# Two transformer layers on one core: the sums of x1, the scaling of its rows and the inner operand parts of the feed-forward at other places in the program

## The chip, the core and the metric

The kernel runs on one core of one Trainium2 chip. The metric is the device time of one execution in microseconds (us), and of several executions the median. A core has a matrix engine (PE in the profile; its weight loads are PEld), a vector engine (DVE), a scalar engine (ACT), a general engine (POOL), and a queue engine that only issues transfers (SP). Each engine takes its instructions strictly in the order of its own list; engines wait for each other by semaphores. PE reads its operands from the on-chip memory SBUF and writes into eight accumulation banks; ACT and DVE read the banks back.

## The reference

Two layers run over 512 positions of 1024 channels. Each has a token mixer of three branches, and then the part that matters here: a norm, a gated feed-forward and a second norm.

```
mix = merged @ w_out[l]
x   = layer_norm(DEEPNORM_ALPHA * x + mix, ln1_g[l], ln1_b[l])
u   = x @ w_ffn_in[l];  u_gate, u_up = split(u)       # 1024 x 2*2816
ffn = (silu(u_gate) * u_up) @ w_ffn_out[l]            # 2816 x 1024
x   = layer_norm(DEEPNORM_ALPHA * x + ffn, ln2_g[l], ln2_b[l])
```

All arithmetic is float32, and the kernel keeps it so.

## The kernel before, in words

**Pairs.** PE multiplies in a shorter format. So every operand is carried as a pair: a high part `hi` (a cast, on ACT) and a low part `lo` (the source minus the high part, on DVE). One product step is three matmuls (`mm3`, L122 to L124): high by high, low by high, high by low. `split` makes a pair from a source (`part_hi` L106 and L108, `part_lo` L112 and L114).

**Products by seven.** Most of the feed-forward is not multiplied plainly. A problem of two by two blocks is computed with seven block products in place of eight, by Winograd's scheme; the names of the seven are m1, m2, y, x, g, h and v. Each needs block sums of both operands. On the weight side `Adds` and `Chain` form these sums in the staging buffers of the weights: with a DVE addition (L241, L246), or with a second load that accumulates onto the buffer (`more`, issued on POOL's queue). On the activation side `Quarters.turned` (L316 to L319) forms four sums of the quarters of x1, transposed, and splits them into the pairs `s12` and `s43`.

**The inner side** (x1 by `w_ffn_in`) has 22 tiles of 128 hidden columns. Sixteen are done by four such problems (`ffn_problem`, four tiles each). Two plain tiles come ahead of them (`u_ffn_first`, tiles 16 and 17), and four more (`u_ffn`, tiles 18 to 21) are put between later products. **The outer side** (hidden by `w_ffn_out`) has two problems, the groups 0 and 1 (`fout_items`), and a rest. The operand parts of an outer problem are made by `Hidden`: its methods y, m1, m2, x, g, v and h form a block sum of the hidden values and split it into the pairs `hq`.

**What sets the order.** The program is a list of items, each with the weights that it needs and a function that emits its products. `run_items` fetches weights until three stand ready, and calls the item. A fetch emits the load (on SP's queue), the high part (L292 or L154, ACT) and the low part (L293 or L155, DVE). Other work is hung on an item as groups of functions: `between()` pops the next group, and an item calls it after each of its products. So in `item(*pr[name], [], todo)` the empty group is popped after the first product and `todo` after the second. From this program order a scheduler makes the list of each engine; it may move instructions past each other where their data allow it.

**Around the change.** In `u_ffn_first` the two plain tiles are multiplied in halves of the positions: first positions 0 to 255 for eight k steps, with a hook ahead of the fifth step that emits the last transposes of x1 (`transposes(3)`, `to_T(1)`), then positions 256 to 511 tile by tile. `ffn_done` makes the hidden pair of a tile. `x1_sums` emits for each of four k the four sums of `turned`, two high parts and two low parts. `natural(t)` scales and shifts one block of 128 rows of x1 (four DVE operations over 128x512: L549, L550) and stores it (two transfers on SP's queue); those rows are the residual of the second norm. `load_res` loads them again as eight pieces of 256 KB, and `plus` adds the outer products to them on DVE. `REST` is 16, `GROUPS` is `[(0, 4), (8, 4)]`; group 0 reads the hidden values of the inner problems 0 and 1.

Of the kernel before, what the change touches and what calls it, by code (L numbers as in the profile page):

```python
# [20 lines left out]
NT = S // P  # L21
KT = D // P
# [28 lines left out]

GROUPS = [(0, 4), (8, 4)]
REST = 16


@with_exitstack
def trunk(ctx, tc, x_in, xT_in, w_in, ret_norm_g, da_norm_g, lq1, lk1, lq2, lk2, w_a, w_b, w_c, b_merge, w_out,
# [13 lines left out]
    saved = [dram.tile([S, D], F32, name=f"saved{i}") for i in range(2 * DEPTH - 1)]  # L71
# [287 lines left out]
    def proj_T(act, wt, c0, nk=KT, ps=None, half=None):  # L359

        ps = bank("pt") if ps is None else ps
        sl = slice(0, S) if half is None else slice(256 * half, 256 * half + 256)
        for k in range(nk):
            a = act[k]
            mm3(ps[:, sl], wt.hi[:, k, c0:c0 + P], wt.lo[:, k, c0:c0 + P], a.hi[:, sl], a.lo[:, sl],
                k == 0, k == nk - 1)
        return ps
# [188 lines left out]
    def item(specs, fn, *groups):  # L556

        items.append((specs, fn, groups))
# [3 lines left out]
    def between():  # L562

        if pending:
            for fn in pending.pop(0):
                fn()
# [54 lines left out]
    def layer(l):  # L621
# [7 lines left out]
        v = {}  # L629
# [520 lines left out]
        x1, x1f = {}, {}  # L1150
# [5 lines left out]
        def load_res(src):  # L1156
            x1["z"] = [[g(name="z") for _ in range(2)] for _ in range(NT)]
            for t in range(NT):
                load_rows(x1["z"][t], src[P * t:P * t + P])
# [58 lines left out]
        def x1_sums():  # L1218
            for k in range(4):
                x1q[k] = Quarters(x1T[k], x1T[k + 4])  # L1220
                x1q[k].turned(x1f.pop(k), x1f.pop(k + 4))

        def u_ffn_first(ids):
            def fn(*wts):
                n = len(ids)
                pg, pu = [bank("pt") for _ in range(n)], [bank("pt") for _ in range(n)]
                proj_T_half0(x1T, [(wts[i], P * j, p[i]) for i in range(n) for j, p in enumerate((pg, pu))],
                             {KT // 2: lambda: (x1["n"].transposes(3), x1["n"].to_T(1))})
                for i in range(n):
                    proj_T(x1T, wts[i], 0, ps=pg[i], half=1)  # L1230
                    proj_T(x1T, wts[i], P, ps=pu[i], half=1)
                    ffn_done(ids[i], pg[i], pu[i])
                    if i == 0:
                        x1_sums()
                for t in range(NT):
                    x1["n"].natural(t)
            return [ffn_spec(i) for i in ids], fn

        def u_ffn(i):
            def fn(wt):  # L1240
                pg = proj_T(x1T, wt, 0)
                pu = proj_T(x1T, wt, P)
                ffn_done(i, pg, pu)
            return [ffn_spec(i)], fn

        def ffn_problem(p):

            hv = Adds(w_ffn_in[l], 0, 4, (512 * p, FFN + 512 * p))
            Z, Y, t = [None] * 2, [None] * 2, {}

            def it(name, use):
                def fn(wt):
                    for b in range(2):
                        use(b, functools.partial(product_T, x1q, name, b, wt))
                        between()
                return [getattr(hv, name)], fn  # L1260

            def copy(to, b, ps):
                t[to, b] = g(name="f" + to)
                nc.scalar.copy(t[to, b], ps)

            def gated(src):
                th = g(name="fth")
                nc.scalar.activation(th, src, AF.Tanh, scale=0.5)
                nc.vector.scalar_tensor_tensor(th, th, 1.0, src, op0=ALU.add, op1=ALU.mult)
                return th  # L1270

            def m1(b, run):
                Z[b] = run()
                copy("m", b, Z[b])

            def m2(b, run):
                m = t.pop(("m", b))
                nc.vector.tensor_add(m, m, run())
                unit[p, 0, b] = gated(m)

            def y(b, run):
                Y[b] = run()

            def x(b, run):
                copy("u", b, run(Z[b], False))

            def gg(b, run):
                copy("w", b, run(Z[b], False))
                w = t["w", b]
                nc.vector.tensor_add(w, w, Y[b])  # L1290

            def h(b, run):
                th = unit[p, 1, b] = gated(run(Z[b], False))
                nc.vector.tensor_mul(th, th, t.pop(("w", b)))

            def v(b, run):
                u, th = t.pop(("u", b)), unit[p, 0, b]
                nc.vector.tensor_add(u, u, run(Y[b], False))
                nc.vector.tensor_mul(th, th, u)

            use = {"m1": m1, "m2": m2, "y": y, "x": x, "g": gg, "h": h, "v": v}
            return {"a": hv.ahead_a, "c": hv.ahead_c, **{k: it(k, fn) for k, fn in use.items()}}
# [68 lines left out]
        def fout_items(gi):  # L1371

            r0, kh = GROUPS[gi]
            hv = Chain(w_ffn_out[l], r0, kh)
            Z, Y, hd = [None] * 2, [None] * 2, {}

            def begin():
                hd["h"] = Hidden(r0 // 4)
                if gi == 0:
                    load_res(saved[2 * l])  # L1380
                    x2["fresh"] = {(t, hf) for t in range(NT) for hf in range(2)}

            def part(name):
                return lambda: getattr(hd["h"], name)()

            def run(name, j, wt, *to):
                return product([hd["h"].row(k) for k in range(kh)], name, j, wt, *to)

            def it(name, use):
                def fn(wt):  # L1390
                    for j in range(2):
                        use(j, functools.partial(run, name, j, wt))
                        between()
                return [getattr(hv, name)], fn

            def y(j, run):
                Y[j] = run()
                plus(2 + j, 1, Y[j], ALU.subtract)

            def m1(j, run):  # L1400
                Z[j] = run()
                plus(j, 0, Z[j], ALU.add)

            def m2(j, run):
                plus(j, 0, run(), ALU.add)

            def x(j, run):
                plus(j, 1, run(Z[j], False), ALU.subtract)

            def gg(j, run):  # L1410
                plus(2 + j, 1, run(Z[j], False), ALU.subtract)

            def v(j, run):
                plus(j, 1, run(Y[j], False), ALU.subtract)

            def h(j, run):
                plus(2 + j, 0, run(Z[j], False), ALU.add)

            use = {"y": y, "m1": m1, "m2": m2, "x": x, "g": gg, "v": v, "h": h}
            return {"a": hv.ahead_a, "c": hv.ahead_c, "begin": begin, "part": part,  # L1420
                    **{k: it(k, fn) for k, fn in use.items()}}

        def fout_rest(hf):
# [32 lines left out]

            return [([sp], block(kb)) for kb, sp in enumerate(specs)] if hf == 0 else [(specs, chase)]

        probs = [ffn_problem(p) for p in range(REST // 4)]
        outs = [fout_items(gi) for gi in range(len(GROUPS))]  # L1460
        item(*u_ffn_first([REST, REST + 1]), [probs[0]["a"], probs[0]["c"]])
        for p, pr in enumerate(probs):
            nxt = probs[p + 1] if p + 1 < len(probs) else outs[0]
            for name in ("m1", "m2", "y", "x", "g", "h", "v"):
                todo = {"g": [nxt["a"]], "v": [nxt["c"]]}.get(name, [])
                if nxt is outs[0]:
                    todo = todo + {"v": [nxt["begin"], nxt["part"]("y"), nxt["part"]("m1")]}.get(name, [])
                item(*pr[name], [], todo)
        rest = list(range(REST + 2, FT))
        for gi, o in enumerate(outs):  # L1470
            nxt = outs[gi + 1] if gi + 1 < len(outs) else None
            order = ("y", "m1", "m2", "-", "x", "g", "v", "-", "h")
            names = [n for n in order if n != "-"]
            for name in order:
                if name == "-":
                    item(*u_ffn(rest.pop(0)))
                    continue
                n = names.index(name) + 2
                todo = [o["part"](names[n])] if n < len(names) else []
                if nxt:  # L1480
                    todo += {"v": [nxt["a"]], "h": [nxt["c"], nxt["part"]("m1")]}.get(name, [])
                    if name == "v":
                        todo += [nxt["begin"], nxt["part"]("y")]
                item(*o[name], todo)
# [61 lines left out]
```

## Time and profile before

| what | us |
|---|---|
| median of three runs | 1926.54 (1925.36 to 1927.0) |
| the profiled execution, its own time | 1925.41 |
| its span, first to last instruction | 1923.6 |
| PE busy | 1885.2 (98%) |
| PEld busy | 1640.2 (85%) |
| DVE busy | 1388.2 (72%) |
| ACT busy | 963.6 (50%) |
| POOL busy | 101.5 (5%) |
| granted PE clock, mean | 0.99 of full |

Times inside the profile count from the first instruction. A wait row says which instruction an engine stood in front of, which instruction released it, the sum of the waits in us, how many there were and the longest. A row of the stretches view gives, for a stretch of time, the busy time of each engine with the number of its instructions, then the granted PE clock, the share of the transfer engines that was busy, and what they moved. A timeline row gives start, duration, engine, source line, operation and tiles, and behind it in brackets the idle time of the engine ahead of it with what ended it. Durations of neighbours on one engine can overlap by some 0.1 us, so the step from one to the next is read from their starts. The program's two layers show the same stretches about 957 us apart.

### The profile page before, as it was taken

How to read it: one execution, taken by the hardware profiler on the slowest of the kernel's cores; microseconds unless marked ns; L12 is line 12 of the kernel's file. 1: busy time of each engine (PE TensorE's matmuls, PEld its weight loads, DVE VectorE, ACT ScalarE, POOL GpSimd, SP SyncE). 2: the span in 40 equal slices, each digit the busy share in tenths (PEclk: the TensorE clock that was granted, in tenths of full speed). 3: DMA queues.
4: the chain of work that ended last, by engine and by line, in shares of the span. 5: the costliest groups of instructions: out<-in, count | busy, mean ns of one | idle time of the engine just before them, and what ended most of it. 6: DMA issues, size and time to landing. Idle time of an engine off the chain costs nothing. (4 is left out here: it accounts for less than half of the span.)

```text
span 1923.6 us, 26474 instructions
## 1 busy us (share of the span) xinstructions
PE 1885.2 (98%) x10354; PEld 1640.2 (85%) x10354; DVE 1388.2 (72%) x2111; ACT 963.6 (50%) x1559; POOL 101.5 (5%) x117
## 2 busy tenths in 40 slices
PE   9999999999999899899999999999999998999998
PEld 7788888888888899888898788888888888998886
DVE  5878866677666977777578788566675759777766
ACT  5555555576534544444255556455765344444441
POOL 0000000000001000010000000000000000000000
PEclk9999999999999899999999999999999998999999
DMA  8585443332264575975556844522422646769851
GB/s 277 168 265 152 133 158 115 99 121 78 72 213 110 155 196 154 252 187 152 153 171 174 254 125 142 185 84 94 132 66 71 218 106 177 175 175 241 197 153 44
DMA packets 221746, 297.85 MB, mean 155 GB/s; under 512 B 9534, under 2 KB 116148, under 8 KB 221620
## 3 DMA queue, kind: packets, MB, share of 16 engines
q1 hardware_dynamic: 198388, 250.01, 39.3%
q0 software_dynamic: 23232, 46.14, 13.8%
q8 instruction: 81, 1.33, 0.3%
q14 instruction: 45, 0.37, 0.1%
HBM read 273.00 MB, written 23.12 MB: 154 GB/s over the span
## 5 line engine op out<-in xcount | busy, mean ns | idle before, releaser
L122 PE MATMUL pt<-xTh,wh 128*128 128x512 f32 (+1 forms) x1456 | 506.1, 348 | 0.4 <-ACT wh L154 0.3
L123 PE MATMUL pt<-xTl,wh 128*128 128x512 f32 (+1 forms) x1456 | 502.5, 345 | 1.9 <-DVE xTl L112 1.9
L124 PE MATMUL pt<-xTh,wl 128*128 128x512 f32 (+1 forms) x1456 | 502.2, 345 | 0.0
L293 DVE TENSOR_TENSOR wl<-st,wh 128x2048 fp32r<-128x2048 f32 x126 | 288.4, 2289 | 120.0 <-ACT wh L292 118.3
L292 ACT CAST wh<-st 128x2048 fp32r<-128x2048 f32 x126 | 240.6, 1910 | 234.3 <-PE pt L123 153.0
L123 PEld LDWEIGHTS pt<-xTl,wh 128*128 128x128 f32 x1456 | 276.1, 190 | 34.1 <-DVE xTl L112 2.3
L124 PEld LDWEIGHTS pt<-xTh,wl 128*128 128x128 f32 x1456 | 275.7, 189 | 33.7
L122 PEld LDWEIGHTS pt<-xTh,wh 128*128 128x128 f32 x1456 | 275.7, 190 | 33.0 <-ACT wh L154 1.0
L154 ACT CAST wh<-st 128x1024 fp32r<-128x1024 f32 (+1 forms) x204 | 187.6, 948 | 183.6 <-issue 70.1
L155 DVE TENSOR_TENSOR wl<-st,wh 128x1024 fp32r<-128x1024 f32 (+1 forms) x204 | 219.0, 1094 | 82.0 <-ACT wh L154 75.9
L122 PE MATMUL pf<-wh,hqh 128*128 128x512 f32 x224 | 89.7, 400 | 5.4 <-ACT hqh L108 5.4
L124 PE MATMUL pf<-wh,hql 128*128 128x512 f32 x224 | 89.1, 399 | 3.4 <-DVE hql L114 3.4
L123 PE MATMUL pf<-wl,hqh 128*128 128x512 f32 x224 | 88.9, 397 | 0.0
L122 PE MATMUL pt<-s12h,wh 128*128 128x256 f32 x256 | 74.6, 296 | 9.5 <-ACT s12h L106 9.5
L123 PE MATMUL pt<-s12l,wh 128*128 128x256 f32 x256 | 75.7, 296 | 3.0 <-DVE s12l L112 3.0
L124 PE MATMUL pt<-s12h,wl 128*128 128x256 f32 x256 | 74.8, 292 | 0.0
L122 PE MATMUL pt<-s43h,wh 128*128 128x256 f32 x256 | 72.4, 283 | 0.0
L123 PE MATMUL pt<-s43l,wh 128*128 128x256 f32 x256 | 72.4, 283 | 0.0
L124 PE MATMUL pt<-s43h,wl 128*128 128x256 f32 x256 | 72.4, 283 | 0.0
L396 ACT COPY sw<-pt 32x512 f32<-32x512 f32 (+1 forms) x96 | 55.6, 579 | 31.4 <-PE pt L124 30.1
L122 PEld LDWEIGHTS pt<-s12h,wh 128*128 128x128 f32 x256 | 51.2, 202 | 10.5 <-ACT s12h L106 10.5
L122 PEld LDWEIGHTS pf<-wh,hqh 128*128 128x128 f32 x224 | 43.3, 193 | 16.1 <-ACT hqh L108 5.8
(294 smaller groups left out, 3897.6 us busy)
## 6 DMA issues: line engine op xcount, KB each, us to landing
st<-in_w_in SPq DMA_DIRECT2D x60, 1024.0 KB
st<-in_w_ffn_in SPq DMA_DIRECT2D x40, 1024.0 KB
st<-in_w_ffn_out SPq DMA_DIRECT2D x24, 1024.0 KB
st<-in_w_in SPq DMA_DIRECT2D x32, 512.0 KB
st<-in_w_ffn_in POOLq DMA_DIRECT2D x16, 1024.0 KB, 9.4
st<-in_w_ffn_out POOLq DMA_DIRECT2D x16, 1024.0 KB, 10.4
st<-in_w_in POOLq DMA_DIRECT2D x12, 1024.0 KB, 11.4
th<-th SPq DMA_DIRECT2D x48, 256.0 KB
```

Of the source, the lines that this page charges most:

```text
L122: nc.tensor.matmul(ps, lh, rh, start=start, stop=False, skip_group_check=more)
L123: nc.tensor.matmul(ps, lh, rl, start=False, stop=False, skip_group_check=more)
L124: nc.tensor.matmul(ps, ll, rh, start=False, stop=stop, skip_group_check=more)
L154: return [nc.scalar.copy(self.hi[:, a:b], self.st[:, a:b]), nc.vector.tensor_sub(self.lo[:, a:b], self.st[:, a:b], f(self.hi[:, a:b]))]
L155: nc.vector.tensor_sub(self.lo[:, a:b], self.st[:, a:b], f(self.hi[:, a:b]))]
L292: nc.scalar.copy(self.hi, st)
L293: nc.vector.tensor_sub(self.lo, st, f(self.hi))
L396: nc.scalar.copy(sw[half * b:half * b + half], ps[half * o:half * o + half])
```

## The change

Four things move. No engine has an instruction more or fewer: PE 10356, DVE 2113, ACT 1369, POOL 122 and SP 482 of the shown kinds stand in both programs.

1. The sums of x1 (`x1_sums`) are emitted in the hook, right behind the transposes, and no longer behind the first plain tile.
2. The scaling of the x1 rows (`natural`) is emitted in four parts, one behind each of the products m1, m2, y and g of the first inner problem (`NATURAL`), and no longer as one block at the end of `u_ffn_first`.
3. `begin` and the y part of outer group 0 hang on product h of the last inner problem, one product earlier than before; its m1 part stays on v.
4. In group 0 the plain tile that stood between m2 and x stands ahead of y, between the inner and the outer side. The loading of the residual rows (`rows`, taken out of `begin`) is emitted between the two halves of this tile (`between()` in `u_ffn`).

```
+NATURAL = ("m1", "m2", "y", "g")
...
-                             {KT // 2: lambda: (x1["n"].transposes(3), x1["n"].to_T(1))})
+                             {KT // 2: lambda: (x1["n"].transposes(3), x1["n"].to_T(1), x1_sums())})
                 for i in range(n):
                     proj_T(x1T, wts[i], 0, ps=pg[i], half=1)
                     proj_T(x1T, wts[i], P, ps=pu[i], half=1)
                     ffn_done(ids[i], pg[i], pu[i])
-                    if i == 0:
-                        x1_sums()
-                for t in range(NT):
-                    x1["n"].natural(t)
...
                 pg = proj_T(x1T, wt, 0)
+                between()
                 pu = proj_T(x1T, wt, P)
...
             def begin():
                 hd["h"] = Hidden(r0 // 4)
-                if gi == 0:
-                    load_res(saved[2 * l])
-                    x2["fresh"] = {(t, hf) for t in range(NT) for hf in range(2)}
+
+            def rows():
+                load_res(saved[2 * l])
+                x2["fresh"] = {(t, hf) for t in range(NT) for hf in range(2)}
...
+                if p == 0 and name in NATURAL:
+                    todo = todo + [functools.partial(natural, NATURAL.index(name))]
                 if nxt is outs[0]:
-                    todo = todo + {"v": [nxt["begin"], nxt["part"]("y"), nxt["part"]("m1")]}.get(name, [])
+                    todo = todo + {"h": [nxt["begin"], nxt["part"]("y")], "v": [nxt["part"]("m1")]}.get(name, [])
                 item(*pr[name], [], todo)
...
-            order = ("y", "m1", "m2", "-", "x", "g", "v", "-", "h")
+            order = (("-", "y", "m1", "m2", "x", "g", "v", "-", "h"), ("y", "m1", "m2", "-", "x", "g", "v", "-", "h"))[gi]
             names = [n for n in order if n != "-"]
-            for name in order:
+            for at, name in enumerate(order):
                 if name == "-":
-                    item(*u_ffn(rest.pop(0)))
+                    item(*u_ffn(rest.pop(0)), *([[o["rows"]]] if at == 0 else []))
```

**Place 1: DVE at the sums of x1, layer 0.** `sa` and `sb` are the sums, `s12l` and `s43l` their low parts; `wl` is the low part of a weight, and `st` on the left is a sum formed in a staging buffer. Before, this stood in a row, from the weight of product y on:

```order
L293 TENSOR_TENSOR wl_5845<-st_5832,wh_5844 128x2048
L112 TENSOR_TENSOR s12l_5703<-sa_5696,s12h_5702 128x512
L241 TENSOR_TENSOR st_5832<-st_5832,st_5902 128x2048
L112 TENSOR_TENSOR s43l_5705<-sb_5697,s43h_5704 128x512
L316 TENSOR_TENSOR sa_5710<-xf_5440,xf_5416 128x256
L319 TENSOR_TENSOR sb_5711<-xf_5416 128x256
L317 SCALAR_TENSOR_TENSOR sa_5710<-xf_5416,sa_5710 128x256
L246 TENSOR_TENSOR st_5838<-st_5838,st_5832 128x2048
L318 SCALAR_TENSOR_TENSOR sb_5711<-sa_5710,xf_5440 128x256
L293 TENSOR_TENSOR wl_5906<-st_5832,wh_5905 128x2048
L112 TENSOR_TENSOR s12l_5717<-sa_5710,s12h_5716 128x512
L293 TENSOR_TENSOR wl_5968<-st_5835,wh_5967 128x2048
```

Now the sums of the four k follow each other, and the first weight behind them is that of m2:

```order
L113 TENSOR_TENSOR s43l_5615<-sb_5607,s43h_5614 128x512
L317 TENSOR_TENSOR sa_5620<-xf_5446,xf_5422 128x256
L320 TENSOR_TENSOR sb_5621<-xf_5422 128x256
L318 SCALAR_TENSOR_TENSOR sa_5620<-xf_5422,sa_5620 128x256
L319 SCALAR_TENSOR_TENSOR sb_5621<-sa_5620,xf_5446 128x256
L113 TENSOR_TENSOR s12l_5627<-sa_5620,s12h_5626 128x512
L294 TENSOR_TENSOR wl_5817<-st_5814,wh_5816 128x2048
L113 TENSOR_TENSOR s43l_5629<-sb_5621,s43h_5628 128x512
```

The five passes over 2048 columns that stood among the sums (for y, x and g, and the two additions) now stand behind them.

**Place 2: DVE at the weight of product h of the first inner problem, now.** `z` are the rows of x1 (scaled and shifted), `fm`, `fth` and `fw` belong to the problem's products, and L247 is the addition that forms the weight block of h; it is the L246 of the first list above.

```order
L550 TENSOR_TENSOR z_5134<-z_5134,bc_5148 128x512
L551 TENSOR_TENSOR z_5136<-z_5136,bc_5152 128x512
L551 TENSOR_TENSOR z_5134<-z_5134,bc_5152 128x512
L550 TENSOR_TENSOR z_5135<-z_5135,bc_5149 128x512
L550 TENSOR_TENSOR z_5137<-z_5137,bc_5149 128x512
L551 TENSOR_TENSOR z_5135<-z_5135,bc_5153 128x512
L551 TENSOR_TENSOR z_5137<-z_5137,bc_5153 128x512
L247 TENSOR_TENSOR st_5814<-st_5814,st_5808 128x2048
L1288 TENSOR_TENSOR fw_6100<-fw_6100,pt_5959 128x512
L294 TENSOR_TENSOR wl_6017<-st_5814,wh_6016 128x2048
L294 TENSOR_TENSOR wl_6073<-st_5884,wh_6072 128x2048
```

The addition for h stood ahead of all scaling before; now twelve of the sixteen scaling operations stand ahead of it.

**Place 3: ACT at the first product of outer group 0.** `wh` are high parts of weights, `hqh` high parts of operand parts. Before, with the weight of y in the first row, that of m1 in the second and that of m2 in the fourth:

```order
L292 CAST wh_7393<-st_7390 128x2048
L1264 COPY fw_7387<-pt_7129 128x512
L1268 ACTIVATE fth_7422<-pt_7102 128x512
L292 CAST wh_7456<-st_7454 128x2048
L1268 ACTIVATE fth_7450<-pt_7129 128x512
L292 CAST wh_7553<-st_7551 128x2048
L108 ACTIVATE hqh_7535<-sy_7531 128x512
L108 ACTIVATE hqh_7539<-sy_7532 128x512
```

Now, with the second half of the plain tile's weight in the first row and the weight of y in the third:

```order
L155 CAST wh_7394<-st_7393 128x1024
L1266 ACTIVATE fth_7426<-pt_7102 128x512
L293 CAST wh_7470<-st_7390 128x2048
L1266 ACTIVATE fth_7454<-pt_7129 128x512
L109 ACTIVATE hqh_7462<-sy_7458 128x512
L109 ACTIVATE hqh_7466<-sy_7459 128x512
L293 CAST wh_7540<-st_7538 128x2048
L109 ACTIVATE hqh_7530<-fth_5917 128x512
```

The y parts now stand ahead of the weights of m1 and m2, and the products of the plain tile (48 matmuls over 512 columns) stand between product v and product y on PE.

More of the change, by code (lines that the diff above doesn't have):

```diff
@@ L1419, in fout_items @@
             use = {"y": y, "m1": m1, "m2": m2, "x": x, "g": gg, "v": v, "h": h}
-            return {"a": hv.ahead_a, "c": hv.ahead_c, "begin": begin, "part": part,
+            return {"a": hv.ahead_a, "c": hv.ahead_c, "begin": begin, "rows": rows, "part": part,
                     **{k: it(k, fn) for k, fn in use.items()}}
@@ L1457, in fout_rest, with natural @@
             return [([sp], block(kb)) for kb, sp in enumerate(specs)] if hf == 0 else [(specs, chase)]
+        def natural(t):
+            x1["n"].natural(t)
         probs = [ffn_problem(p) for p in range(REST // 4)]
```

## The prediction

> **What bounds the kernel now.** I read the page's head first, then the waits of PE, then stretches around the waits, and last the timelines of DVE and ACT there.
>
> ```profile
> span 1923.6 us, 26474 instructions
> PE 1885.2 (98%) x10354; PEld 1640.2 (85%) x10354; DVE 1388.2 (72%) x2111; ACT 963.6 (50%) x1559; POOL 101.5 (5%) x117
> ```
>
> PE is busy 98% of the span, so only what keeps PE waiting, or slows it, is to be won. Its waits, longest first (us in total, times, longest):
>
> ```profile
> PE pt L122 <- ACT s12h L106: 9.5, 4, 3.7
> PE pf L122 <- ACT hqh L108: 5.4, 2, 2.7
> PE pf L124 <- DVE hql L114: 3.4, 2, 2.1
> PE pt L123 <- DVE s12l L112: 3.0, 2, 1.5
> PE pt L123 <- DVE xTl L112: 1.9, 2, 1.0
> PE psr L122 <- DVE rtmp L822: 1.6, 1, 1.6
> ```
>
> The two `s12` rows are product y of the first inner problem, which waits for the sums of x1; the two `hq` rows are product y of outer group 0, which waits for its operand parts. Together 21.3 us over both layers. The change is aimed at these four places and at no other. What they cost in all is shown by the stretches from the start of each of the four products to the start of the next, with an undisturbed product of each kind behind them and, last, a plain tile:
>
> ```profile
> core 0: us, PE busy (x) PEld busy (x) DVE busy (x) ACT busy (x) POOL busy (x), PEclk, DMA share, GB/s
> 637.59:653.33 15.74, 9.51 (x51) 8.36 (x49) 14.43 (x22) 6.78 (x10) 1.31 (x1) 0.67 0.78 200
> 797.33:810.67 13.34, 8.50 (x27) 6.33 (x25) 11.62 (x17) 5.24 (x7) 0.00 (x0) 0.74 1.11 253
> 1594.50:1611.24 16.74, 10.50 (x51) 9.35 (x49) 15.43 (x24) 6.78 (x10) 1.31 (x1) 0.69 0.75 189
> 1755.23:1767.56 12.33, 8.35 (x26) 6.12 (x25) 11.24 (x17) 5.24 (x7) 0.00 (x0) 0.72 1.12 243
> 653.33:659.09 5.76, 5.76 (x51) 5.76 (x49) 5.76 (x11) 3.55 (x4) 0.00 (x0) 1.00 0.37 140
> 810.67:816.11 5.44, 5.44 (x26) 4.50 (x24) 4.83 (x7) 3.05 (x4) 0.00 (x0) 1.00 0.25 88
> 821.55:832.43 10.88, 10.88 (x50) 9.01 (x48) 4.84 (x6) 2.51 (x2) 1.03 (x1) 1.00 0.85 193
> ```
>
> An inner product takes 5.76 us, an outer one 5.44. So the four lose 9.98, 7.90, 10.98 and 6.89: **35.75 us**. PE is idle for 58.15 - 36.86 = 21.29 of it, the sum of the wait rows; the other 14.5 is the clock, 0.67 to 0.74 in these rows and 1.00 in the others.
>
> What is late in the first place? DVE, not a transfer:
>
> ```profile
> 634.72 2.28 DVE L246 TENSOR_TENSOR st<-st 128x2048 f32<-128x2048 f32 x1
> 636.92 0.42 DVE L318 SCALAR_TENSOR_TENSOR sb<-sa,xf 128x256 f32<-128x256 f32 x1
> 637.25 2.28 DVE L293 TENSOR_TENSOR wl<-st,wh 128x2048 fp32r<-128x2048 f32 x1
> 639.46 0.68 DVE L112 TENSOR_TENSOR s12l<-sa,s12h 128x512 fp32r<-128x512 f32 x1
> 640.06 2.28 DVE L293 TENSOR_TENSOR wl<-st,wh 128x2048 fp32r<-128x2048 f32 x1
> 643.53 0.41 DVE L317 SCALAR_TENSOR_TENSOR sa<-xf,sa 128x256 f32<-128x256 f32 x1
> ...
> 643.98 0.62 ACT L106 CAST s12h<-sa 128x512 fp32r<-128x512 f32 x1 [3.85 <-DVE sa L317]
> ```
>
> Product y starts at 637.59 and needs the sums of all four k; the third comes at 643.53, because passes over 2048 columns (2.2 us each, by the starts) stand among the sums.
>
> **The change part by part.** I take DVE passes at the steps of these starts: 2.21 us for 2048 columns, 0.60 for 512 (639.46 to 640.06).
>
> *Sums first.* All sums now stand ahead of the passes for y, x and g. The last one waits for the high part of y's weight, which stands before it on ACT and waits for PE to leave a buffer:
>
> ```profile
> 626.15 1.91 ACT L292 CAST wh<-st 128x2048 fp32r<-128x2048 f32 x1 [3.33 <-PE pt L123]
> 633.28 1.92 ACT L292 CAST wh<-st 128x2048 fp32r<-128x2048 f32 x1 [4.18 <-DVE st L241]
> ```
>
> That wait is PE's own progress (the second plain tile ends), and it stays: high part done at 628.06, y's low part on DVE until 630.3, the last s12 low part at 630.9. Product y starts at 637.59, so 6.7 us of cover. The 9.98 and 10.98 us go. The sums also step in among the last transposed pieces of x1:
>
> ```profile
> 613.92 0.42 DVE L112 TENSOR_TENSOR xTl<-xf,xTh 128x256 fp32r<-128x256 f32 x1 [0.45 <-ACT xTh L106]
> 614.55 0.28 PE L122 MATMUL pt<-xTh,wh 128*128 128x256 f32 x1
> ```
>
> The last piece, done at 614.34, gets one ACT cast and one DVE pass put ahead of it, 1.1 us. PE begins the second half at 614.55 and comes to that piece 22 matmuls later, 617.2: 1.7 us of cover, so nothing.
>
> *Where the stall goes.* The DVE work is not less, so I count on. From 628.06 to the addition that forms h's weight block (place 2 of the order) DVE has 5 passes over 2048 columns, that addition among them, and 24 over 512 columns, 12 of them row scaling: 5 x 2.21 + 24 x 0.60 = 25.5, to 653.5. On the way x's low part is done at 641.3 (needed 643.4) and g's at 643.5 (needed 649.1): in time. Then ACT makes h's high part (1.91, to 655.4) and DVE its low part (2.28, to 657.7). Product h is due at 637.59 + 3 x 5.76 = 654.87. Only five matmuls can be done without the low part (0.6 us), so PE waits about 657.9 - 654.87 - 0.6 = **2.4 us a layer**. Before, the addition was done at 634.72, and this wait did not exist; the moved scaling (12 x 0.60 = 7.2 us ahead of it) makes it. Bounds: nothing, if DVE runs 2.4 us ahead of my count; 3.9 with a slow clock, below. I take 2.4, since each duration in the count stands in a row.
>
> *The clock.* The four stretches lost (1 - 0.67) x 15.74 / 0.5 = 10.4 us, 6.9, 10.4 and 6.9 at half clock; the smallest step between these is 3.45 us. At half clock an inner product's step is 0.213 instead of 0.12:
>
> ```profile
> 651.09 0.41 PE L123 MATMUL pt<-s12l,wh 128*128 128x256 f32 x1
> 651.31 0.41 PE L124 MATMUL pt<-s12h,wl 128*128 128x256 f32 x1
> ...
> 652.14 0.28 PE L124 MATMUL pt<-s12h,wl 128*128 128x256 f32 x1
> 652.26 0.28 PE L122 MATMUL pt<-s12h,wh 128*128 128x256 f32 x1
> ```
>
> So one such step after the new wait would cost 3.45 x (1 - 0.12 / 0.213) = 1.5 us a layer. Waits of 1.0 and 1.6 us stand in the rows of waits; around the latter the clock stayed up:
>
> ```profile
> 1086.00:1094.00 8.00, 6.12 (x30) 5.00 (x29) 6.91 (x7) 7.05 (x9) 0.00 (x0) 1.00 0.20 49
> ```
>
> The new wait is broken by the five matmuls into pieces of 0.6, 1.5 and 0.3 us. The longest piece of the new wait is nearest to these, so I take no slow clock. [...]
>
> *Scaling spread.* Its 16 operations are the same. Its stores go out on SP between weight loads, which stand behind them: the next problem's m1 weight can be loaded when the addition for h leaves its buffer, at 653.5. At the 140 GB/s of the 653.33 row, 1 MB takes 7.5 us: 661.0, high part 662.9, low part 665.2. It is due at 637.59 + 5 x 5.76 + 2.4 = 668.8. Cover 3.6 us; every us beyond it would cost one.
>
> *Outer group 0.* Before, the parts came behind the last low parts and gated products on DVE:
>
> ```profile
> 797.59 0.68 DVE L1299 TENSOR_TENSOR fth<-fth,fu 128x512 f32<-128x512 f32 x1
> 798.79 0.68 DVE L1334 TENSOR_TENSOR sy<-fth 128x512 f32<-128x512 f32 x1
> 802.79 0.68 DVE L114 SCALAR_TENSOR_TENSOR hql<-sy,hqh 128x512 fp32r<-128x512 f32 x1
> ...
> 793.45 0.59 ACT L1268 ACTIVATE fth<-pt 128x512 f32<-128x512 f32 x1
> ```
>
> Now the y part follows the last tanh of product h (794.05): one pass of 2.21 and five of 0.60 to the last low part, 799.3. The plain tile is 10.88 us (its row above; the same tile leaves its old place, so PE's work is unchanged), and y starts at 797.33 + 10.88 = 808.2. Cover 8.9 us: the 7.90 and 6.89 go.
>
> What loses its cover is x, which had the tile ahead of it, and m2. From m2's high part (it waits until the tile leaves its buffer at 808.2, then 1.91) DVE has m2's, x's and g's low parts (6.6) and eleven passes over 512 columns (6.6) to x's first low part: 810.1 + 13.2, with 0.8 of waits for PE results among them 824.1, due 824.53 + 0.45. In the same count m2's is ready at 819.5, due 820.0. Bounds: nothing, or about 1 us at each; I take **0.4 us a layer**.
>
> *Residual rows.* Eight loads:
>
> ```profile
> 784.84 5.75 SPq L468 DMA_DIRECT2D z<-saved  x8
> 808.20 0.69 DVE L1309 SCALAR_TENSOR_TENSOR z<-z,pf 128x512 f32<-128x512 f32 x1 [1.72 <-PE pf L124]
> ```
>
> Before, they were issued within 5.75 us, and their first user waited for PE alone. Now the last five wait on SP for a buffer that the last gated product frees at about 796, and the first user comes at 808.2 + 2.7 + its queue, 812.9: 17 us. The five rows, the 1-MB weight load ahead of them and the accumulating load of that time are 3.4 MB, 13.4 us at the 253 GB/s of the 797.33 row. Hidden; the cover is 3.5 us.
>
> Sum: 35.75 - 2 x 2.4 - 2 x 0.4 = 30.15. The profiled execution took 1925.41, so 1895.3; the median shown is 1.1 above that execution: **1896.4**.
>
> **The rivals.**
> 1. *The wait at h does not arise.* For it: DVE's count has no slack built in, but ACT and DVE overlap by 0.1 us at each hand-over. Against: it needs 2.4 us of 25.5. Time 1926.54 - 35.75 = 1890.8.
> 2. *The chain through DVE slips further*, at h (late by 4 to 5 us, with one or two slow steps of the clock) or at m2 and x (1 us each): 30.15 - 2 x (2 + 1.5) to - 2 x 1.5, so 1899 to 1904. For it: DVE is busy 14.43 of 15.74 us in that stretch, so a single late hand-over moves all behind it.
> 3. *The waits only move.* The gap at y opens again at m1' or at x, and half of the gain is lost: 1910. Against: the covers counted above, 3.5 us and more.
> 4. *Slower: the residual rows land late.* DVE's first addition to a row stands ahead of the operand parts of m2, so each us that a row lands behind 812.9 stops PE for one. To be slower than before it must be over 15 us late in each layer, at 828 or later, 32 us after the issue; landing at 831 would give 1932. For it: the transfer engines had no time left in the 797.33 row (share 1.11). Against: at 253 GB/s the 32 us carry 8 MB, more than twice what is to be moved.
>
> **How the numbers follow.** Forecast 0.60 (1893 to 1899), rival 1 0.13, rival 2 0.17, rival 3 0.05, rival 4 0.03, and 0.02 that the change does nothing that shows. A measurement of this kernel tells about 0.2%, 3.9 us, from no change. Faster: the first three, rival 3, 0.95; same 0.02; slower 0.03. The range takes rivals 1 and 2 in: 1890 to 1904.
>
> **What would show it.** In the waits of PE: no `s12h`, `s12l`, `hqh` or `hql` rows of over 0.5 us; a new row for L123 or L125 of product h, <- ACT or DVE `wh`, `wl`, about 2 us a layer. The granted clock 1.00 through all four stretches, DVE's addition for h near 653. I am wrong if PE still waits for `s12`, if the clock falls after the wait at h, or if a row <- DMA appears on DVE at the first additions of group 0.

## The result, and the profile after

The changed kernel takes 1898.46 us (median of four runs, 1896.01 to 1899.83) against 1926.69 of the kernel before (the three runs shown above and a fourth): ratio 0.9853, 95% interval 0.9836 to 0.987. The forecast was 1896.4 us. The profiled execution took 1897.19 of its own time, 28.2 us less than the profiled execution before; the sum in the prediction was 30.15.

The page of the changed kernel, its head:

```profile
span 1895.4 us, 26476 instructions
PE 1874.2 (99%) x10354; PEld 1634.1 (86%) x10354; DVE 1386.7 (73%) x2111; ACT 962.8 (51%) x1559; POOL 101.5 (5%) x117
```

The work is the same. PE's busy time fell by 11.0 us. The half clock accounts for some 8 of it: before, it lasted 10.24, 6.83, 10.24 and 6.83 us in the four stretches, and PE was busy for 25.1 us of that; now it lasts 3.41 us twice, with PE busy for 6.5. A matmul's step in it is 0.213 us instead of 0.12. The rest of the 11.0 was not traced. The waits of PE in the changed kernel (total us, times, longest):

```profile
PE pt L123 <- ACT wh L293: 3.8, 4, 1.3
PE pt L124 <- DVE xTl L113: 1.9, 2, 1.0
PE pf L123 <- ACT s43h L107: 1.6, 1, 1.6
PE psr L123 <- DVE rtmp L823: 0.8, 1, 0.8
```

All `s12` and `hq` rows of over 0.5 us are gone. The longest row is new: `wh` at L293 is the high part of a weight, and its four waits are the two products h and v of the first inner problem, once a layer. (The changed program is one line longer: L293 here is L292 before, L247 is L246, and so on.) The stretches from product to product in the changed kernel show what is left at the old places: product x; then g, that is up to the start of h; then from h to the next problem's m1, two products together; for layer 1 from y to h, three products, and again from h to m1; and last, of outer group 0, the stretches of y, of m2, of x and of g:

```profile
642.79:648.55 5.76, 5.76 (x50) 5.76 (x49) 5.76 (x11) 1.82 (x3) 0.00 (x0) 1.00 0.58 186
648.55:655.10 6.55, 5.92 (x50) 5.72 (x48) 5.12 (x7) 3.13 (x4) 1.31 (x1) 1.00 0.85 203
655.10:669.85 14.75, 13.45 (x97) 13.17 (x98) 11.69 (x12) 7.02 (x6) 1.28 (x1) 0.88 0.93 294
1579.56:1597.62 18.06, 17.44 (x146) 17.23 (x145) 16.64 (x21) 9.42 (x12) 1.31 (x1) 1.00 0.55 147
1597.62:1612.18 14.56, 13.26 (x97) 13.06 (x97) 12.00 (x12) 7.03 (x6) 0.29 (x1) 0.88 0.97 313
801.71:807.15 5.44, 5.44 (x25) 4.51 (x24) 3.48 (x4) 2.40 (x2) 0.00 (x0) 1.00 0.80 247
812.59:818.21 5.62, 5.62 (x26) 4.43 (x24) 5.62 (x8) 2.96 (x3) 0.63 (x1) 1.00 0.78 132
818.21:824.04 5.83, 5.60 (x26) 4.35 (x24) 5.83 (x8) 3.16 (x4) 0.00 (x0) 1.00 0.81 237
824.04:829.58 5.54, 5.54 (x24) 4.59 (x25) 5.17 (x8) 3.90 (x6) 1.28 (x1) 1.00 1.02 281
```

An inner product is 5.76 us, so in layer 0 the start of h is 0.79 late and from h to m1 another 14.75 - 11.52 = 3.23 are lost: 4.02 us. In layer 1 it is 0.78 + 3.04 = 3.82. The clock in both h stretches is 0.88. At group 0 product y loses nothing; m2, x and g lose 0.18, 0.39 and 0.10, and in layer 1 nearly the same (0.17, 0.39 and 0.12). How h comes to be late stands in the timelines of the changed kernel (DVE, ACT, then PE):

```profile
650.77 2.29 DVE L247 TENSOR_TENSOR st<-st 128x2048 f32<-128x2048 f32 x1
655.09 4.49 DVE L294 TENSOR_TENSOR wl<-st,wh 128x2048 fp32r<-128x2048 f32 x2 [1.43 <-ACT wh L293]
...
653.15 3.70 ACT L293 CAST wh<-st 128x2048 fp32r<-128x2048 f32 x2 [0.87 <-DVE st L247]
...
655.10 0.38 PE L123 MATMUL pt<-xTh,wh 128*128 128x256 f32 x1 [0.63 <-ACT wh L293]
655.33 0.28 PE L124 MATMUL pt<-xTl,wh 128*128 128x256 f32 x1
656.90 0.48 PE L123 MATMUL pt<-s43h,wh 128*128 128x256 f32 x1 [1.29 <-ACT wh L293]
...
806.48 0.68 DVE L1307 SCALAR_TENSOR_TENSOR z<-z,pf 128x512 f32<-128x512 f32 x1
```

The addition ends at 653.06, the high part of h at about 655.06, its low part at about 657.3. PE stops ahead of h (0.79 by the stretches), and again from 655.33 to 656.90, where 0.12 is the usual step: there the scheduler put a matmul of v, whose high part is the second of the two casts on ACT. With some 0.2 us more at the low part, the wait is 2.5 us a layer. The last row is the first addition to a residual row: it waited for no transfer, and no DVE row from 800 to 830 us waits for one.

### The profile page after: what moved, and what is told of

Its sections match the earlier page's. It is cut to its first block, busy times and chain, and to the rows that moved or that the text cites. A ratio compares the mean times of both kernels' runs of the same rounds, so it can differ in the third digit from the quotient of the medians.

```text
span 1895.4 us, 26476 instructions
## 1 busy us (share of the span) xinstructions
PE 1874.2 (99%) x10354; PEld 1634.1 (86%) x10354; DVE 1386.7 (73%) x2111; ACT 962.8 (51%) x1559; POOL 101.5 (5%) x117
## 5 line engine op out<-in xcount | busy, mean ns | idle before, releaser
L293 ACT CAST wh<-st 128x2048 fp32r<-128x2048 f32 x126 | 240.2, 1910 | 224.7 <-PE pt L124 123.5
L123 PE MATMUL pf<-wh,xTh 128*128 128x512 f32 x144 | 56.3, 391 | 0.3 <-ACT tg L772 0.3
L125 PE MATMUL pf<-wh,xTl 128*128 128x512 f32 x144 | 56.1, 390 | 0.0
```

The lines of the kernel that those rows point to most:

```text
L123: nc.tensor.matmul(ps, lh, rh, start=start, stop=False, skip_group_check=more)
L125: nc.tensor.matmul(ps, ll, rh, start=False, stop=stop, skip_group_check=more)
L293: nc.scalar.copy(self.hi, st)
```

## The experiments

I started from this theory: the four places are independent; each part of the change removed the stall at its own place; the wait at h comes from the scaling passes ahead of the addition; and the rest of the loss at h is a slow clock. Each run is compared with the kernel before on its own chip.

### The inner side alone, the outer side alone

The first kernel takes back parts 3 and 4 (the cut shows its main lines). The second takes back parts 1 and 2, that is, the sums and the scaling stand in `u_ffn_first` as in the kernel before.

```
-                    todo = todo + {"h": [nxt["begin"], nxt["part"]("y")], "v": [nxt["part"]("m1")]}.get(name, [])
+                    todo = todo + {"v": [nxt["begin"], nxt["rows"], nxt["part"]("y"), nxt["part"]("m1")]}.get(name, [])
...
+            order = ("y", "m1", "m2", "-", "x", "g", "v", "-", "h")
```

> Parts 1 and 2 of the change alone: sums of x1 first, row scaling spread; group 0 as before (y part on product v, plain tile between m2 and x, rows loaded in begin). Theory (the four places are independent, each lost its own stall): place A gives 9.98 + 10.98 - 2 x (2.5 wait at h + 1.4 slow clock) = 13.2 us, so 1926.6 - 13.2 = 1913.4; waits of PE show hqh and hql rows of about 8.8 us together and no s12 row. Rival (one stall shields the other: an earlier product y makes group 0 wait longer): 1916 or more, hq rows over 10 us.

> Parts 3 and 4 alone: y part of group 0 a product earlier, plain tile ahead of group 0, rows loaded between the halves of the tile; sums and scaling of x1 as before. Theory of independent places: 7.90 + 6.89 - 1.0 (small waits at m2 and x) = 13.8 us, so 1912.8; s12 rows of about 12.5 us stay, hq rows vanish. Rival (the gain at group 0 is only there because the scaling was moved off DVE): under 8 us of gain, 1919 or more.

Measured: inner side alone 1910.39 us, ratio 0.9923 (0.991 to 0.9935), a gain of 14.9; outer side alone 1913.74, ratio 0.9938 (0.9926 to 0.995), a gain of 11.6. Together 26.5; the whole change gave 28.2. PE's longest waits, first with the inner side alone, then with the outer side alone:

```profile
PE pf L123 <- ACT hqh L109: 5.4, 2, 2.7
PE pt L123 <- ACT wh L293: 3.9, 4, 1.3
PE pf L125 <- DVE hql L115: 3.1, 2, 1.8
```

```profile
PE pt L123 <- ACT s12h L107: 9.5, 4, 3.7
PE pt L124 <- DVE s12l L113: 3.0, 2, 1.5
```

Each half removes its own rows and leaves the others at their old size, and the wait at h belongs to the inner half. Both rivals of these runs (a shield between the stalls, a gain at group 0 that hangs on the scaling) fall; what remains to 28.2 is within the spread of the runs. The sizes were expected less well: 13.2 and 13.8 us of gain, against 14.9 and 11.6.

### The sums late, the scaling spread (part 1 undone)

```
-                             {KT // 2: lambda: (x1["n"].transposes(3), x1["n"].to_T(1), x1_sums())})
+                             {KT // 2: lambda: (x1["n"].transposes(3), x1["n"].to_T(1))})
...
+                    if i == 0:
+                        x1_sums()
```

> The change with part 1 undone: the sums of x1 behind the first plain tile as before, the scaling spread as in the change, parts 3 and 4 kept. Theory (it is the place of the sums that removes the stall at y, the spreading does not): from 628.06 to the last low part of the sums DVE has 5 passes over 2048 columns, 12 over 512 and 12 over 256: 11.1 + 7.2 + 4.4 = 22.7, so 650.8 in place of 630.9; y's last k can start at 650.8 and not at 641.9, so some 8.5 us of wait a layer and three slow steps of 1.5; no wait at h: 1890.7 + 2 x (8.5 + 4) = 1915.7; s12 rows of 15 us or more. Rival (taking the scaling off DVE suffices): s12 rows under 6 us, 1905 or less.

Measured: 1915.94 us, ratio 0.9946 (0.9929 to 0.9962). PE's longest waits:

```profile
PE pt L124 <- DVE s12l L113: 11.6, 4, 3.5
PE pt L123 <- ACT s12h L107: 6.7, 2, 3.5
```

18.3 us of `s12` waits, more than the 12.5 before, since the scaling passes now stand among the sums too. So the stall at y is removed by the place of the sums. Spreading the scaling without it makes the stall longer.

### The sums first, the scaling as one block (part 2 undone), and the scaling in the second problem

```
+                for t in range(NT):
+                    x1["n"].natural(t)
...
-                if p == 0 and name in NATURAL:
+                if False:
```

```
-                if p == 0 and name in NATURAL:
+                if p == 1 and name in NATURAL:
```

> The change with part 2 undone: sums first, but the scaling as one block at the end of the two plain tiles as before; parts 3 and 4 kept. Theory (it is the scaling set ahead of the addition for h that makes the wait at h; the spreading was not needed): the addition for h is back ahead of x's low part, no wait at h and no slow clock, 1898.5 - 2 x (2.5 + 1.4) = 1890.7. By the count of DVE passes from 643.35 on, v's low part would be done at 659.4, due 660.6, so only 1.2 us of cover there. Rival (DVE has no room for the scaling in this problem at all, wherever it stands): the wait moves to v or to the next m1, of 2 us or more a layer, 1895 to 1900.

> The change with the four parts of the scaling behind m1, m2, y and g of the second inner problem instead of the first. Theory (the wait at h comes from 12 scaling passes ahead of the addition in a problem where DVE also has the sums and the hidden values of two plain tiles): wait at h gone in both problems, 1890.7. Rival (the slack of DVE is the same in every problem, the wait only moves): a wait of about 2 us a layer at h of problem 1, 1895 to 1899.

Measured: block 1904.22 us, ratio 0.9889 (0.9874 to 0.9904); second problem 1901.23, ratio 0.9872 (0.9858 to 0.9885). The theory had 1890.7 for both. The block is slower than the change, whose ratio is 0.9836 to 0.987; the second problem is 2.8 us slower, but its interval overlaps that of the change. The wait at h is gone in both, as it should be, but another has come. The run with the scaling in the second problem (PE's longest wait, then ACT, then PE):

```profile
PE pt L123 <- ACT fm L1262: 5.9, 2, 2.9
...
638.25 1.90 ACT L293 CAST wh<-st 128x2048 fp32r<-128x2048 f32 x1
643.97 1.90 ACT L293 CAST wh<-st 128x2048 fp32r<-128x2048 f32 x1 [3.34 <-PE pt L124]
646.31 1.05 ACT L1262 COPY fm<-pt 128x512 f32<-128x512 f32 x2
...
646.93 0.39 PE L123 MATMUL pt<-s12h,wh 128*128 128x256 f32 x1 [2.93 <-ACT fm L1262]
```

Product x accumulates onto the banks of m1, so it waits until ACT has copied m1's result (`fm`). The copy could run long before, since m1's matmuls end two products earlier, but it stands on ACT behind the high part of h's weight, and that cast waits until PE leaves a weight buffer (643.97). With the addition for h early, the scheduler put the cast ahead of the copies; with the addition late, as in the change, behind them. The block version has the same row (5.9 us). So the theory holds for the wait at h and was wrong in what follows when it goes: its place was taken by a wait of 2.9 us a layer at x; the granted clock was 0.996 over both runs, 0.997 over that of the change.

### One block of scaling in the first problem, three in the second

From ACT's list in the built program I chose a placing where the copies of m1 stay ahead of h's high part and few passes stand ahead of the addition.

```
-NATURAL = ("m1", "m2", "y", "g")
+NATURAL = ((0, "m1"), (1, "m1"), (1, "m2"), (1, "x"))
...
-                if p == 0 and name in NATURAL:
-                    todo = todo + [functools.partial(natural, NATURAL.index(name))]
+                if (p, name) in NATURAL:
+                    todo = todo + [functools.partial(natural, NATURAL.index((p, name)))]
```

The second kernel of this pair has `((0, "m1"), (0, "y"), (1, "y"), (1, "x"))` there.

> The change with one of the four blocks of scaling behind m1 of the first inner problem and three behind m1, m2 and x of the second: four scaling passes ahead of the addition for h instead of twelve. On ACT the high part of h's weight stands behind the copies of m1's result then, as in the change, and ahead of the copies of x's result. Theory (the wait at h of the change is the scaling ahead of the addition; the wait at x of the run with all scaling in the second problem is only the high part of h standing ahead of the copies of m1 on ACT): neither wait, 1898.5 - 2 x (2.5 + 1.4) = 1890.7; no half clock in the feed-forward. Rival (DVE or ACT is short of room there whatever the order; the stall goes to g or h): x's second copy stands behind v's high part, done 651.6, due 652.0; if it is late, 1 us or more a layer, 1893 to 1897.

> The change with two blocks of scaling behind m1 and y of the first inner problem and two behind y and x of the second: seven scaling passes ahead of the addition for h. On ACT both copies of x's result stand ahead of h's high part. Theory: addition done 3 us earlier than in the change (five passes of 0.6), h's low part 654.7, due 654.4 + 0.6: no wait or 0.3 us at h, no slow clock, 1890.7 to 1892. Rival (the wait at h does not hang on these passes but on the high part and ACT): wait of 2 us or more stays, 1896 or more.

Measured: one block first 1891.31 us (1890.91 to 1892.3), ratio 0.9819 (0.9804 to 0.9833). It beats both kernels, by 7 us the changed one. Two blocks first: 1907.21, ratio 0.9901 (0.9886 to 0.9916). The first of them, DVE, ACT, and two stretches that begin within product y:

```profile
646.58 2.28 DVE L247 TENSOR_TENSOR st<-st 128x2048 f32<-128x2048 f32 x1
...
642.30 1.06 ACT L1262 COPY fm<-pt 128x512 f32<-128x512 f32 x2
648.95 3.73 ACT L293 CAST wh<-st 128x2048 fp32r<-128x2048 f32 x2 [0.67 <-DVE st L247]
656.30 1.90 ACT L293 CAST wh<-st 128x2048 fp32r<-128x2048 f32 x1 [2.26 <-PE pt L124]
...
641.00:655.00 14.00, 14.00 (x119) 14.00 (x118) 13.17 (x10) 8.96 (x11) 1.31 (x1) 1.00 0.64 183
655.00:680.00 25.00, 25.00 (x211) 25.00 (x210) 20.16 (x21) 11.05 (x10) 1.28 (x1) 1.00 0.79 211
```

The addition runs 4.2 us earlier in the trace than in the change, and 6.0 us earlier counted from the start of product y, which comes 1.8 us later in this trace. The copies of m1 come before the casts, PE is busy without a break and its clock stays at 1.00. This run moves three blocks out of the first problem, so by itself it does not tell order from room on DVE; the two runs before do. The block run keeps all sixteen passes in the problem, behind the addition, and h's low part is done at 649.4 there, 12 us before h starts; and the wait at x came with no scaling in the problem at all. So both waits are a matter of order. The second of them, PE's longest wait and ACT:

```profile
PE pt L123 <- ACT fw L1262: 11.6, 2, 6.2
...
655.73 0.57 ACT L1262 COPY fw<-pt 128x512 f32<-128x512 f32 x1
663.21 1.90 ACT L293 CAST wh<-st 128x2048 fp32r<-128x2048 f32 x1 [6.90 <-DMA st<-in_w_ffn_in]
665.01 0.58 ACT L1262 COPY fw<-pt 128x512 f32<-128x512 f32 x1
```

The wait at h is gone here too: no `wh` row of L293 is left among the waits of PE, and the addition ends 3.0 us earlier than in the change, counted from product y, as expected. But the second copy of g's result (`fw`), for which h waits because it accumulates onto the same bank, stands on ACT behind the high part of the next problem's m1, and that cast waits 6.9 us for its load. In the run with one block the same cast stands at the same place of ACT's list, but its load had landed: it ran at 656.30 and waited for PE alone. I had looked at DVE and at the place of x's copies and not at this cast; the expectation was wrong by 15 us. The load was issued as the addition ended in both runs, at 652.05 here and at 648.89 there; it took 11.2 us here and at most 7.4 there. What slowed it was not tried.

### Group 0: the tile without the early part, the early part without the tile

The first kernel takes back part 3 alone:

```
-                    todo = todo + {"h": [nxt["begin"], nxt["part"]("y")], "v": [nxt["part"]("m1")]}.get(name, [])
+                    todo = todo + {"v": [nxt["begin"], nxt["part"]("y"), nxt["part"]("m1")]}.get(name, [])
```

The second takes back part 4 alone, and loads the residual rows with the y part:

```
-                    todo = todo + {"h": [nxt["begin"], nxt["part"]("y")], "v": [nxt["part"]("m1")]}.get(name, [])
+                    todo = todo + {"h": [nxt["begin"], nxt["rows"], nxt["part"]("y")], "v": [nxt["part"]("m1")]}.get(name, [])
...
-            order = (("-", "y", "m1", "m2", "x", "g", "v", "-", "h"), ("y", "m1", "m2", "-", "x", "g", "v", "-", "h"))[gi]
+            order = ("y", "m1", "m2", "-", "x", "g", "v", "-", "h")
...
```

> The change without part 3: the y part of group 0 hangs on product v again, the plain tile still stands ahead of group 0. Theory (the tile alone covers the lateness at group 0): the parts were at most 4.7 us late before, the tile gives 10.88: same as the change, 1898.5, no hq rows among the waits of PE. Rival (the parts a product ahead do it): hq rows of 2 us or more a layer, 1903 or more.

> The change without part 4: the y part of group 0 a product ahead, the plain tile between m2 and x as before, rows loaded with the y part. Theory (the tile does it): from the last tanh of product h at 794.05, nine DVE passes of 0.60 stand to the first low part of y, 799.4, due 797.33 + 0.6: wait of 1.5 to 2 us a layer at y, none at m2 and x (0.5 less): 1898.5 + 2 x 1.5 = 1901.5, and 1904.3 if the clock falls one step each time. Rival (the earlier part suffices): no hq row over 0.5 us, 1898 or less.

Measured: tile alone 1897.7 us, ratio 0.9858 (0.9842 to 0.9875), the same as the whole change; early part alone 1906.55, ratio 0.9893 (0.9878 to 0.9908). With the early part alone, PE's longest wait, then DVE and ACT ahead of y:

```profile
PE pf L123 <- ACT hqh L109: 5.4, 2, 2.7
...
786.68 2.29 DVE L294 TENSOR_TENSOR wl<-st,wh 128x2048 fp32r<-128x2048 f32 x1 [1.55 <-ACT wh L293]
788.89 0.68 DVE L1267 SCALAR_TENSOR_TENSOR fth<-fth,pt 128x512 f32<-128x512 f32 x1
791.88 1.28 DVE L1332 TENSOR_TENSOR sy<-fth 128x512 f32<-128x512 f32 x2
...
786.55 0.59 ACT L1266 ACTIVATE fth<-pt 128x512 f32<-128x512 f32 x1
792.60 1.23 ACT L109 ACTIVATE hqh<-sy 128x512 fp32r<-128x512 f32 x2 [0.20 <-DVE sy L1332]
```

The wait of 2.7 us a layer is as long as before the change; only the wait for the low parts is gone. I had expected 1.5 to 2 and had left out that the last tanh, done at 787.1, finds DVE in a pass over 2048 columns until 788.9. So at group 0 the tile alone does all of it, and beside the tile part 3 adds nothing that can be measured. Without the tile part 3 is worth something: with neither (the inner side alone) the ratio is 0.9923 in place of 0.9893, and PE waits 3.1 us for the low parts besides.

### The changed kernel twice more

In the run with the tile alone the waits at h are the same, and yet the clock did not fall: behind 3.41 us with PE busy for 1.95 it was 1.00 (656.90 and 660.31 us of that trace). And the changes of the granted clock lie on a grid, in the trace of the kernel before (half clock for 10.24, 6.83, 10.24 and 6.83 us, three and two times 3.413) as in that of the change (3.41 twice). That gave a theory of the clock, tested with two more executions of the unedited change.

> The changed kernel once more, nothing edited, for another position of the same wait at h against the clock. Theory (the clock is decided at the end of every stretch of 3.413 us of a grid that runs by itself, and falls to half for the next one where PE was busy for less than about 0.55 of it): the waits of PE at h are the same 2.5 us a layer as before; in each layer the clock falls after them only if one stretch of the grid shows under 0.55 PE busy; 0, 1 or 2 slow steps at h, own time 1894.4 + 1.4 for each slow step in the whole run. Rival (a wait of this length always, or never, brings the slow clock): one slow step in each layer whatever the grid shows, or none.

> As the run before, for a third position of the grid: same waits at h, 0 to 2 slow steps there by the share that the grid shows, own time 1894.4 + 1.4 a slow step. Rival: always one a layer, or never.

Measured: 1899.56 and 1895.09 us, one execution each. Stretches of that grid around h: first the profiled execution of the change, layer 0; then the first repetition, layer 0 and layer 1; then the second, layer 0. The first figure behind the length is PE's busy time, the third from the end the clock.

```profile
653.62:657.04 3.42, 1.49 (x11) 1.08 (x10) 1.99 (x2) 3.42 (x3) 0.00 (x0) 1.00 1.11 253
657.04:660.45 3.41, 3.41 (x16) 3.33 (x17) 3.41 (x4) 0.29 (x1) 0.00 (x0) 0.50 1.07 324
660.45:663.86 3.41, 3.41 (x31) 3.41 (x30) 0.35 (x2) 1.96 (x2) 0.00 (x0) 1.00 1.05 396
```

```profile
656.20:659.61 3.41, 2.11 (x15) 1.73 (x15) 3.41 (x2) 2.04 (x2) 0.00 (x0) 1.00 1.10 252
659.62:663.03 3.41, 3.41 (x31) 3.41 (x30) 2.06 (x3) 0.00 (x0) 0.00 (x0) 1.00 1.05 396
...
1598.33:1601.75 3.42, 1.49 (x11) 1.08 (x9) 2.04 (x1) 3.42 (x3) 0.00 (x0) 1.00 1.11 249
1601.75:1605.16 3.41, 3.41 (x16) 3.25 (x16) 3.41 (x4) 0.20 (x1) 0.00 (x0) 0.50 1.05 371
```

```profile
652.17:655.59 3.42, 2.46 (x19) 2.04 (x17) 1.99 (x3) 2.80 (x2) 0.00 (x0) 1.00 1.10 241
655.58:659.00 3.42, 2.45 (x18) 2.27 (x19) 3.42 (x2) 1.40 (x2) 0.00 (x0) 1.00 1.08 287
659.00:662.42 3.42, 3.42 (x31) 3.42 (x31) 1.42 (x3) 0.85 (x1) 0.00 (x0) 1.00 1.05 402
```

The same wait, several answers. Where it lies in one stretch (1.49 busy of 3.42, a share of 0.44) the next 3.41 us run at half clock, with 16 matmuls in place of 31. Where the edge of a stretch cuts it (2.46 and 2.45, shares of 0.72) the clock stayed at 1.00. In between, it stayed after 2.11 (0.62) too, while in layer 1 of the profiled execution 1.80 of 3.42 (0.53) was followed by a stretch at 0.50. In layer 1 of the second repetition two stretches around the wait show 2.52 and 2.56 of 3.42, and the clock at 1.00 in both. So the rival, always or never, falls. The second repetition had no slow step, and took 1895.09 where 1894.4 was expected. The first had two, one of them at the head products (L823) behind a stretch with a share of 0.58, a little above the expected 0.55, and took 1899.56 where 1897.2 was expected: by the starts of the same matmuls in both traces, its two slow steps cost 1.6 and 1.3 us, and some 1.2 us had come before them, in the first 80 us of the program. There the second repetition lost 1.9 us, by my estimate to a longer start at half clock (until 10.5 us, against 4.3), while the first had waits of 1.8 and 1.2 us (rows `s43h` and `s43l`, near 70 and 78 us) that the second did not have. Why those two waits come and go is open.

## Why the prediction was right, and where it was off

**Sums first.** Right. Product y of the first problem waits for nothing, and with the sums late again the stall is back, larger (18.3 us).

**The new wait at h.** Right in place, cause and size, though the pieces are not all what was counted. Counted were 653.5 for the addition, 655.4 for the high part, 657.7 for the low part and 2.4 us of wait; the trace has 653.06, 655.06, 657.3 and 2.5. (The 2.4 was worked out from 657.9; from the 657.7 that the count itself gives it is 2.2.) The prediction gave the longest piece to the low part of h; in the trace a matmul of v stands there that waits for its own high part until 656.90, and only 0.2 us fall to the low part, which ends at nearly the same time. The cause is shown by the run with one block ahead of the addition, where the wait is gone and the time is 1891.31; the prediction's first rival, the wait not arising, stood at 1890.8.

**The clock.** This is the step that failed: "I take no slow clock", a term put at nothing. In the profiled execution it fell in both layers, for one step each. From h to m1 3.23 and 3.04 us were lost, of them about 1.45 by the gap from 655.33 and 0.2 at the low part: 1.6 and 1.4 us by the clock, against the bound of 1.5 that the prediction had worked out and set aside. The reason it gave, that the longest piece of the wait is near in length to waits that left the clock alone, was the wrong measure: pieces of 0.63 and 1.29 us that lay in one stretch of the grid left PE busy for 1.49 of its 3.42 us, and the clock fell; cut by an edge, they left 2.46 and 2.45, and it did not. Which of the two it was differed between executions of the same program, so the right term was a chance: two slow steps at h, one, or none in the three traces of the change, 0 to 3 us. With the tile alone, which has the same wait, it was none (granted clock 0.999 over the run). The witness that the prediction chose, the wait at L822 with the clock at 1.00 around it, was such a chance too: at the same wait the clock fell in the first repetition.

**Scaling spread.** The next problem's m1 came without a wait; the counted cover of 3.6 us held. What the prediction did not see is the other side of the spreading: by making the addition late it also kept the cast of h behind the copies on ACT. Taken back, PE waits 2.9 us a layer at x. So the moved scaling was counted as a pure cost, while against the alternative at hand (the block) it brought some 6 to 7 us (5.8 by the medians, 6.9 by the ratios).

**Outer group 0.** Right that the stall goes; 0.18, 0.39 and 0.10 us were lost at m2, x and g, 0.67 in place of 0.4 a layer. The 0.4 was taken between bounds, for the count itself left a little cover at both m2 and x; g was not counted. The reason for the gain was half right: the prediction named the tile's 10.88 us and the earlier part together, and the tile is enough.

**Residual rows.** Right, hidden. No row waits for a transfer at the first additions, and rival 4 did not come.

**The sum.** In place of 4.8 us the two waits at h cost 4.02 + 3.82 = 7.84, of which 3.0 are the clock, and group 0 1.35 in place of 0.8. That alone would have given 26.6; the execution gained 28.2. Of the 1.6 us between, 0.8 is the wait at L823, which changes from execution to execution: 1.6 us before, 0.8 here, and 0.6 to 2.3 in the other runs. The rest was not traced. So that the total came within 2 us of the sum is in part luck: the missing clock term was half made up by gains that nobody had counted.

## What to carry to other kernels

A wait that is removed uncovers what stood behind it in some engine's list, and the list is the scheduler's: after every edit, read on each engine what now stands ahead of the copies that free the accumulation banks, and whether that instruction itself waits for PE or for a load. Count a chain pass by pass, from the instruction that starts it and with the pass that the engine is in at that moment; the chain to h came out within 0.5 us that way, and the expectations that missed had each left out one instruction: the cast ahead of the copies of m1, the cast ahead of the second copy of g, the pass that DVE was in at the last tanh. A single late pass can be worth placing work elsewhere, even a whole problem later: 12 of 16 small passes moved one problem on gave 7 us more than the change itself.

## What was not expected of the hardware

The changes of PE's granted clock lie on a grid. In the trace of the kernel before, all ten fall within 0.01 us of one grid of 3.413 us, and all six in that of the changed kernel do; the position of the grid differs, with one of its edges at 6.72 us from the first instruction before and at 5.09 after. I laid it over these two traces and took PE's busy share of every stretch at full clock. After all seven stretches with a share of 0.11 to 0.44 the clock was at half in the next one, for instance after 1.21 us busy of 3.41 at 798.61 us before; after none of the 13 with 0.64 to 0.84 was it. Of the three in between it fell after one: after 1.80 us (0.53, at 1595.70 after), and not after 1.78 (0.52, at 66.53 after) or 1.93 (0.57, at 1593.92 before). In the last microseconds of the run with the scaling in the second problem, at 1890 us, one stretch with a share of 0.45 did not bring it. From half clock it was back at full after the six stretches with a share of 0.91 to 1.00 and stayed at half after the eight of 0.00 to 0.89 (at 1604.16 us before, 3.03 busy of 3.41). So in these traces a little less than half of a stretch idle was enough, 1.61 us of 3.41 at 1595.70, and it need not be one wait: in layer 0 of the changed kernel it was two, of 0.63 and 1.29 us. The waits at h, 2.5 us a layer, cost 4.02 and 3.82 us where the clock fell behind them, and whether it fell changed from execution to execution.
